# One core, a hybrid encoder block: splits and sums moved between GpSimd, VectorE and ScalarE at four places

## Chip, core and metric

The kernel runs on one core of one Trainium2 chip. The metric is the device time of one execution in microseconds (us). TensorE's clock has two levels, 1.2 and 2.4 GHz; the profile gives the granted clock as a share of the higher one. Engine names in rows: PE is TensorE, DVE is VectorE, ACT is ScalarE, POOL is GpSimd, SP is the sync engine, which issues most DMAs.

## The reference, cut to what matters

```python
h = _rms_norm(x, norm_mix_gain)                       # x is (1, 2048, 1024), float32
proj = h @ w_in                                       # q, k, v (768 columns each) and u (256)
attn = _dilated_attention(q, k, v, rel_bias_table)    # three windows and dilations, 12 heads
four = _fourier_mix(u, fourier_w, fourier_b)
x = x + concat(norm(attn), norm(four)) @ w_out
h = _rms_norm(x, norm_ffn_gain)
g, val = h @ w_gate, h @ w_val                        # D_FF = 2816
g = conv1d(g, conv_w) + conv_b                        # 3 taps along the positions
x = x + (silu(g) * val) @ w_down
return _rms_norm(x) * final_norm_gain
```

## The kernel before

Each float32 operand is split into two float16 parts, a high one (`hi`) and what it leaves (`lo`), and each product is three matmuls: hi·hi, hi·lo, lo·hi (`mm3`). Before a split, a tensor is scaled by a power of two that comes from its largest magnitude; finding it across partitions is a `PARTITION_ALL_REDUCE` on GpSimd (`all_max`). A split is an ACTIVATE on ScalarE (hi) and a subtraction (lo), on VectorE as one SCALAR_TENSOR_TENSOR that scales too (`split`), or on GpSimd as a TENSOR_TENSOR on data scaled beforehand. Every engine runs its own instructions in program order; pools give buffers and the waits on them.

- **Input projection** (`project`, 0 to some 180 us). The 2048 tokens go through in four quarters `c` of 512. For each there are four products V (values, two tokens blocks of 256 in halves `a`), two U (Fourier input) and sixteen Q (queries and keys). `hooks` lists, per quarter and product, which other work is emitted behind it. In quarter 0 the x rows 0 and 1 and rows 2 and 3 are normalized and turned apart (`half_turn`), the V weights `wv` are split partly on GpSimd, the Fourier weights `wf` and the first query and key weights `wqk` also.
- **Attention, Fourier, output projection** (to 1041.5 us, when the first gate product starts), not touched.
- **Gate and value tiles** (`glu`, 22 tiles `j`, to 1891.6 us). Seven half-size products stand for eight; `bank` holds X, Y, Z, W in PSUM, and `prod(n, a, b)` is 24 matmuls. Tile 20 also finds the last maxima of the down weights (`down_scale`, whose staging buffer `dws` is single) and starts the first down weights (`down_first`); tile 21 is `last_tile`, which ends in the largest magnitude `a_lm` that scales the down products.
- **Down, first half** (`down`, to 2010 us): 512 tokens, eleven steps `k` of two parts `i` with 24 matmuls each. During step `k` the weights of `k + 1` are split (`down_parts`) and their four sums made (`down_sums`) and split.
- **Down, second half** (to the end): 66 steps of 21 matmuls, seven products of three each; `last` adds the last seven up, normalizes and stores two blocks of 128 tokens.

Of the kernel before, what the change touches and what calls it, by code (L numbers as in the profile page):

```python
# [20 lines left out]
D = 1024  # L21
# [77 lines left out]
class Staged:  # L99
# [36 lines left out]

    def split(self, w, c0=0):
# [15 lines left out]
class Block:  # L153
# [47 lines left out]
    def rstd(self, ss, dim, name, unit2=None, width=None):  # L201
# [11 lines left out]
        nc.scalar.activation(y, v, AF.Sqrt)  # L213
        r = new("_r")
# [195 lines left out]
    def project(self, pv):  # L410
# [19 lines left out]
        def norm(c, js):  # L430
            r = self.rstd(stat[c][:, js[0]:js[-1] + 1], D, "xr", width=4)
            for i, j in enumerate(js):
                nc.vector.tensor_scalar(rows[c][j], rows[c][j], r[:, i:i + 1], None, op0=OP.mult)
# [3 lines left out]

        def half_turn(k, h):

            self.to_T([x[:, k * 128:(k + 1) * 128] for x in rows[0][2 * h:2 * h + 2]], self.hT, k, 1, R_MIX + k, self.mmtile,  # L440
                      2 * h, 2)
# [14 lines left out]
        load(0, (0, 1), nc.scalar)  # L456
# [4 lines left out]
        wv = self.staged("w_in", 2 * AW, "wv")  # L461
        load(0, (2, 3))
        wf = self.staged("w_in", 3 * AW, "wf")
# [4 lines left out]
        next(gains)  # L468
        wv.bound(w[:, 0])
        for k in range(KT):  # L470
            half_turn(k, 0)
            if k == 0:
                wv.root()
                nc.gpsimd.tensor_tensor(wv.st[:, 6:], wv.st[:, 6:], wv.s[:, 0:1, None].to_broadcast([128, 8 - 6, 256]),
                                        op=OP.mult)
            if k == 3:
                nc.scalar.activation(w[:, 0, :6], wv.st[:, :6], AF.Copy, scale=wv.s[:, 0:1])
            if k == 3:
                nc.vector.scalar_tensor_tensor(w[:, 1, :6], wv.st[:, :6], wv.s[:, 0:1], w[:, 0, :6], op0=OP.mult,
                                               op1=OP.subtract)  # L480
        nc.scalar.activation(w[:, 0, 6:], wv.st[:, 6:], AF.Copy)
        nc.gpsimd.tensor_tensor(w[:, 1, 6:], wv.st[:, 6:], w[:, 0, 6:], op=OP.subtract)
        squares(0, (2, 3))
        norm(0, (2, 3))


# [5 lines left out]

        def first_f():
            self.finv = self.const.tile([128, 1], F32, name="finv")
            nc.vector.tensor_copy(self.finv, wf.inv)
            wf.split(halves(W["f"]))

        def bound_f():
# [1712 lines left out]
```

## Time and profile before

| | |
|---|---|
| time, median of 3 runs | 2333.05 us (2329.04 to 2335.33) |
| the profiled execution: its time, and its span | 2329.35 us, 2327.5 us |
| TensorE busy | 2227.7 us, 96% of the span |
| VectorE, ScalarE, GpSimd busy | 71%, 43%, 31% |
| mean granted clock | 0.989 |

The span runs from the first to the last instruction; some 1.9 us lie around it. Busy shares are means over the whole; where a wait ends last is read stretch by stretch.

### The profile page before, as it was taken

To read this page: it belongs to the slowest core of one execution; us is meant where nothing else is said; L and a number is where in the kernel's file an instruction comes from. 1 tells how busy PE (TensorE), PEld (TensorE's weight loads), DVE (VectorE), ACT (ScalarE), POOL (GpSimd) and SP (SyncE) were. 2 spreads that over 40 slices of the span, in tenths; PEclk is the share of its full clock that TensorE was granted. 3 is DMA by queue.
4 is the path that set the end of the run, shared out by engine and by line. 5 is a ranking of instruction groups with operands and counts; after the bars stand their busy time and mean duration, and the time that the engine had idled before them with its cause. 6 is when DMAs were issued, how large, how long until landed. Compare 5 with 4: busy or idle time off the path is not lost.

```text
span 2327.5 us, 39297 instructions
## 1 busy us (share of the span) xinstructions
PE 2227.7 (96%) x15173; PEld 1199.0 (52%) x15173; DVE 1654.1 (71%) x3372; ACT 1007.4 (43%) x1841; POOL 730.7 (31%) x692
## 2 busy tenths in 40 slices
PE   5999999999999988999999999999999989999997
PEld 3657866666666654544444444444444434444443
DVE  4656768788787889863787877877778579654454
ACT  5433468677776764543222222222222144432222
POOL 1112122343443423231121221212212236566665
PEclk9999999999999998999999999999999999999998
DMA  3434334353543796960213222121221334443322
GB/s 134 144 102 125 119 105 122 81 139 84 156 124 111 219 286 201 276 178 13 73 55 100 68 78 91 46 91 57 80 91 46 100 118 136 135 137 96 95 91 82
DMA packets 281706, 266.47 MB, mean 114 GB/s; under 512 B 62102, under 2 KB 244014, under 8 KB 280494
## 3 DMA queue, kind: packets, MB, share of 16 engines
q1 hardware_dynamic: 276302, 245.60, 35.5%
q10 hardware_dynamic: 5216, 18.35, 2.2%
q8 instruction: 119, 1.95, 0.4%
q14 instruction: 69, 0.57, 0.1%
HBM read 176.32 MB, written 86.27 MB: 113 GB/s over the span
## 4 chain that ended last, share of the span: by engine, by line
issue 21%; PE 15%; POOL 9%; DVE 7%; ACT 4%; DMA 0%; POOLq 0%; ACTq 0%; SPq 0%; DVEq 0%
POOL A L1823 6%; PE d L241 4%; PE d L239 4%; PE d L240 4%; ACT A L1822 2%; PE X L1634 1%; DVE wst_v L1798 1%; DVE wd L192 1%; PE Z L1634 1%; ACT wd L191 1%; POOL sums L1908 1%; POOL sums L1907 1%; POOL sums L1906 1%; POOL sums L1905 1%; DVE wst_v L1802 0%
## 5 line engine op out<-in xcount | busy, mean ns | idle before, releaser
L1634 PEld LDWEIGHTS <-A 128*128 128x128 f16 x3744 | 366.6, 98 | 456.0 <-issue 16.2
L1002 ACT ACTIVATE s_sb<-s_sb,R 128x256 f32<-128x256 f32 (+1 forms) x576 | 229.7, 456 | 122.1 <-DVE R L994 121.4
L994 DVE CUSTOM_DVE_ANT_0 s_sb<-s,bias,alpha 128x256 f32<-128x256 f32 (+1 forms) x576 | 217.2, 420 | 77.6 <-PE s L989 76.9
L1634 PE MATMUL X<-h2T,A 128*128 128x512 f16 x1092 | 243.2, 379 | 1.7 <-DVE x L1529 1.7
L1634 PE MATMUL W<-h2T,A 128*128 128x512 f16 x984 | 220.6, 381 | 5.6 <-DVE gt L1728 5.6
L1634 PE MATMUL Y<-T,A 128*128 128x512 f16 x960 | 213.7, 379 | 4.5 <-DVE h2T L1653 2.2
L1823 POOL TENSOR_TENSOR A<-wst_v,A 128x2048 f16<-128x2048 f32 (+3 forms) x46 | 153.4, 3348 | 182.1 <-ACT A L1822 134.9
L241 PE MATMUL d<-wd,aT 128*128 128x512 f16 x540 | 204.7, 379 | 5.0 <-DVE aT L192 5.0
L239 PE MATMUL d<-wd,aT 128*128 128x512 f16 x540 | 204.7, 379 | 0.0
L240 PE MATMUL d<-wd,aT 128*128 128x512 f16 x540 | 204.7, 379 | 0.0
L192 DVE SCALAR_TENSOR_TENSOR aT<-wst_v,a_s,aT 128x896 f16<-128x896 f32 x66 | 86.9, 1316 | 145.6 <-ACT aT L191 145.6
L1014 DVE SCALAR_TENSOR_TENSOR pT<-pt,pT 128x512 f16<-128x512 f32 (+1 forms) x240 | 156.8, 653 | 15.9 <-ACT pT L1009 15.4
L191 ACT ACTIVATE aT<-wst_v,a_s 128x896 f16<-128x896 f32 x66 | 68.7, 1040 | 193.6 <-PE d L241 114.5
L165 POOL PARTITION_ALL_REDUCE wg_a<-am_g x22 | 8.2, 372 | 458.7 <-DVE am_g L1790 446.7
L241 PE MATMUL mm<-hT,wqk 128*128 128x512 f16 x384 | 146.4, 381 | 5.5 <-POOL wqk L642 5.5
L239 PE MATMUL mm<-hT,wqk 128*128 128x512 f16 x384 | 147.4, 384 | 2.7 <-ACT wqk L641 2.7
L1007 PE MATMUL pt<-eye,s_sb 128*128 128x128 f32 x900 | 148.0, 285 | 0.1
L1009 ACT ACTIVATE pT<-pt 128x512 f16<-128x512 f32 (+1 forms) x240 | 135.9, 566 | 24.7 <-PE pt L1007 16.0
L240 PE MATMUL mm<-hT,wqk 128*128 128x512 f16 x384 | 146.3, 381 | 0.0
L239 PE MATMUL av<-vb,pT 128*128 128x65 f16 (+1 forms) x960 | 116.3, 197 | 28.1 <-ACT R L1030 27.6
L1822 ACT ACTIVATE A<-wst_v 128x2048 f16<-128x2048 f32 (+3 forms) x46 | 73.1, 1593 | 158.0 <-DVE wst_v L1798 135.5
L1840 DVE SCALAR_TENSOR_TENSOR act<-gt,cw,act 128x2047 f32<-128x2047 f32 x22 | 81.9, 3723 | 60.4 <-ACT act L1837 60.4
(476 smaller groups left out, 4824.4 us busy)
## 6 DMA issues: line engine op xcount, KB each, us to landing
a_d<-val SPq DMA_DIRECT2D x42, 512.0 KB, 3.5
wst_v<-a_d SPq DMA_DIRECT2D x66, 256.0 KB, 3.3
vb<-v_d SPq DMA_DIRECT2D x12, 1040.0 KB
wst_v<-w_gate SPq DMA_DIRECT2D x22, 512.0 KB
wst_v<-w_val SPq DMA_DIRECT2D x44, 256.0 KB, 5.2
dws<-w_down SPq DMA_DIRECT2D x22, 512.0 KB, 6.0
wst_v<-w_down SPq DMA_DIRECT2D x11, 1024.0 KB, 5.0
Ro<-acc_d SPq DMA_DIRECT2D x36, 264.0 KB
```

The lines of the kernel that those rows point to most:

```text
L192: nc.vector.scalar_tensor_tensor(lo, src, scale, hi, op0=OP.mult, op1=OP.subtract)
L239: t.matmul(out, lh, rh, start=first, stop=False)
L240: t.matmul(out, lh, rl, start=False, stop=False)
L241: t.matmul(out, ll, rh, start=False, stop=last)
L994: nc.vector.tensor_tensor_reduce(s_sb[:, o:o + wd], s_ps[:, o:o + wd], bias[:, h, bc:bc + wd], alpha[:, 1:2], 3.0e38, OP.add, OP.min, nm)
L1002: nc.scalar.activation(s_sb[:, o:o + wd], s_sb[:, o:o + wd], AF.Exp, scale=-1.0, bias=nm)
L1007: nc.tensor.transpose(pt[:, o:o + 128], keep["p"][:, o:o + 128], self.eye)
L1009: nc.scalar.activation(pT[:, 0, :tot], pt[:, :tot], AF.Copy, scale=2.0 ** 14)
L1014: nc.vector.scalar_tensor_tensor(pT[:, 1, :tot], pt[:, :tot], 2.0 ** 14, pT[:, 0, :tot], op0=OP.mult, op1=OP.subtract)
L1634: nc.tensor.matmul(out[:, c - cols.start:c - cols.start + 512], A[:, a, x, k], B[b][:, y, k, c:c + 512], start=first and k == 0 and (x, y) ...
L1822: self.nc.scalar.activation(hi, src, AF.Copy)
L1823: self.nc.gpsimd.tensor_tensor(lo, src, hi, op=OP.subtract)
```

## The change

In the head all four x row tiles and both weight tiles are loaded by the ScalarE queue; the rows are turned 512 tokens at a time; `wv`, `wf` and the first `wqk` are scaled and split by ScalarE and VectorE alone (`direct`, `qk_direct`), and two small memsets go from GpSimd to VectorE. In gate tile 20 the sum that empties bank W stands ahead of the last `down_scale`. In `last_tile` the first down weights are split behind the first gate half (`next(first)`), the `a_max` part before the gate. In the first down half the four sums are made on VectorE, behind the splits; the x tiles are loaded one step part earlier than `load_f(2)`. In the last two steps of the down part the products of p1, p6, p7 and p5 go first, and `last` is written in another order with fewer GpSimd operations. Diff, cut (`down_sums` now takes the engine; `rstd` takes `during`; `half_turn` is gone):

```diff
+    def direct(self, w):
+        n, s = w.shape[2] // 2, self.s[:, 0:1]
+        for k in (slice(0, n), slice(n, 2 * n)):
+            self.b.nc.scalar.activation(w[:, 0, k], self.st[:, k], AF.Copy, scale=s)
+            yield
+            self.b.nc.vector.scalar_tensor_tensor(w[:, 1, k], self.st[:, k], s, w[:, 0, k], op0=OP.mult, op1=OP.subtract)
+            yield
...
         nc.scalar.activation(y, v, AF.Sqrt)
+        if during:
+            during()
...
-        load(0, (0, 1), nc.scalar)
+        load(0, range(4), nc.scalar)
         gains = self.gains(True)
         next(gains)
         self.eye = self.const.tile([128, 128], F32, name="eye")
         self.dma(self.eye, io["c_eye"])
-        wv = self.staged("w_in", 2 * AW, "wv")
-        load(0, (2, 3))
-        wf = self.staged("w_in", 3 * AW, "wf")
+        wv = self.staged("w_in", 2 * AW, "wv", nc.scalar)
+        wf = self.staged("w_in", 3 * AW, "wf", nc.scalar)
         next(gains)
         w = pv.tile([128, 2, KT, 256], F16, name="w_v")
         squares(0, (0, 1))
         norm(0, (0, 1))
-        next(gains)
+        squares(0, (2, 3))
+        norm(0, (2, 3), lambda: next(gains))
         wv.bound(w[:, 0])
+        first = [self.mmtile() for k in range(KT)]
+        for h in range(2):
+            for k in range(KT):
+                for j in (2 * h, 2 * h + 1):
+                    nc.tensor.transpose(first[k][:, j * 128:(j + 1) * 128], rows[0][j][:, k * 128:(k + 1) * 128], self.eye)
+        wv.root()
+        part = wv.direct(w)
         for k in range(KT):
-            half_turn(k, 0)
-            if k == 0:
-                wv.root()
-                nc.gpsimd.tensor_tensor(wv.st[:, 6:], wv.st[:, 6:], wv.s[:, 0:1, None].to_broadcast([128, 8 - 6, 256]),
-                                        op=OP.mult)
-            if k == 3:
-                nc.scalar.activation(w[:, 0, :6], wv.st[:, :6], AF.Copy, scale=wv.s[:, 0:1])
-            if k == 3:
-                nc.vector.scalar_tensor_tensor(w[:, 1, :6], wv.st[:, :6], wv.s[:, 0:1], w[:, 0, :6], op0=OP.mult,
-                                               op1=OP.subtract)
-        nc.scalar.activation(w[:, 0, 6:], wv.st[:, 6:], AF.Copy)
-        nc.gpsimd.tensor_tensor(w[:, 1, 6:], wv.st[:, 6:], w[:, 0, 6:], op=OP.subtract)
-        squares(0, (2, 3))
-        norm(0, (2, 3))
+            self.split(self.hT[:, 0, k, :512], self.hT[:, 1, k, :512], first[k], self.gs[:, R_MIX + k:R_MIX + k + 1])
+            if k % 2:
+                next(part)
+        load(1)
+        self.qk_load(0)
...
+        def bound_f():
+            W["f"] = xr.tile([128, 2, KT, 256], F16, name="wf")
+            wf.bound(W["f"][:, 0])
         def first_f():
+            wf.root()
             self.finv = self.const.tile([128, 1], F32, name="finv")
             nc.vector.tensor_copy(self.finv, wf.inv)
-            wf.split(halves(W["f"]))
-        def bound_f():
-            W["f"] = xr.tile([128, 2, KT, 256], F16, name="wf")
-            wf.bound(W["f"][:, 0]).root()
+            for _ in wf.direct(W["f"]):
+                pass
         def next_load():
             W["1"] = self.staged("w_in", 2 * AW + 256, "w1")
@@ -506,15 +513,15 @@
             W["1"] = W["1"].split(halves(pv.tile([128, 2, KT, 256], F16, name="w_v")))
         gains = self.gains(False)
-        at(0, "V", 0, bound_f, *(lambda k=k: half_turn(k, 1) for k in range(KT)))
-        at(0, "V", 1, lambda: next(gains), lambda: self.qk_load(0), lambda: load(1), wf.scale, first_f)
-        at(0, "V", 2, self.qk_bound)
-        at(0, "V", 3, lambda: self.qk_scale(0), lambda: self.qk_split(0, False), lambda: self.qk_split(1, False), lambda: next(gains))
+        bound_f()
+        at(0, "V", 0, first_f, lambda: next(gains))
+        at(0, "V", 1, self.qk_bound)
+        at(0, "V", 3, lambda: self.qk_scale(0, False), lambda: self.qk_direct(), lambda: next(gains))
         for c in range(3):
             if c:
                 at(c, "V", 0, lambda c=c: load(c + 1))
-            at(c, "V", 3, lambda c=c: squares(c + 1, range(4)))
-            at(c, "U", 0, lambda c=c: norm(c + 1, range(4)))
+            at(c, "V" if c else "U", 3 if c else 0, lambda c=c: squares(c + 1, range(4)))
+            at(c, "U", 0 if c else 1, lambda c=c: norm(c + 1, range(4)))
...
-                nc.gpsimd.memset(self.v_r[:, :, :, HD:HD + 1], 1.0)
-                nc.gpsimd.memset(self.v_r[:, :, :, VW - 1:VW], 0.0)
+                nc.vector.memset(self.v_r[:, :, :, HD:HD + 1], 1.0)
+                nc.vector.memset(self.v_r[:, :, :, VW - 1:VW], 0.0)
...
-        for i in range(2):
+        self.qk_s = s
+        for i in range(2 if weights else 0):
             nc.vector.tensor_scalar(st[:, i], st[:, i], s[:, i:i + 1], None, op0=OP.mult)
...
+    def qk_direct(self):
+        for i in range(2):
+            w, st, s = self.wq[i], self.qk_w[:, i], self.qk_s[:, i:i + 1]
+            self.nc.scalar.activation(w[:, 0], st, AF.Copy, scale=s)
+            self.nc.vector.scalar_tensor_tensor(w[:, 1], st, s, w[:, 0], op0=OP.mult, op1=OP.subtract)
...
+                prod("W", 6, "22")
+                tt_(u1, bank["W"], u1, op=add)
                 if j == NF - 2:
                     self.down_scale(gp, j + 1)
                     first = self.down_first()
                     next(first)
-                prod("W", 6, "22")
-                tt_(u1, bank["W"], u1, op=add)
                 past = self.glu_act(ga, j, gt, val, inv)
...
+            if n == "X":
+                next(first)
...
+        [*first]
...
-            if c == 1:
-                [*first]
...
-        _, ap = self.pow2(am[:, :NK], 0, "amx", NK)
+        am = self.all_max(am[:, :NK], "amx", NK)
+        yield
+        _, ap = self.pow2(am, 0, "amx", NK, reduced=True)
...
-                        self.down_sums(fs[k + 1], g)
-                        self.down_parts(k + 1, fs.pop(k + 1), w[k + 1], b12[k + 1])
+                        self.down_parts(k + 1, fs[k + 1], w[k + 1], b12[k + 1])
+                        self.down_sums(fs.pop(k + 1), g, nc.vector)
                     elif i == 0:
+                        x = [x_tile(t) for t in range(2)]
...
-                add(x2[:, hi], z)
+                onto(x2[:, hi], p5, x2[:, hi])
+                tt(x2[:, hi], x2[:, hi], z, op=OP.add)
+                square(0, x2[:, hi])
+                tt(x2[:, lo], x2[:, lo], z, op=OP.add)
                 onto(x1[:, hi], p5, x1[:, hi])
-                add(x2[:, lo], z)
-                onto(x2[:, hi], p5, x2[:, hi])
+                onto(x1[:, hi], p3, x1[:, hi])
+                square(1, x1[:, hi])
                 onto(x1[:, lo], p2, x1[:, lo])
-                onto(x1[:, hi], p3, x1[:, hi])
+                square(2, x1[:, lo])
                 onto(x2[:, lo], p4, x2[:, lo], neg)
-                for i, y in enumerate((x2[:, hi], x1[:, lo], x1[:, hi], x2[:, lo])):
-                    sq = other().bitcast(BF16)
-                    nc.scalar.activation(sq[:, :512], y, AF.Square, accum_out=ss[:, i:i + 1])
-                nc.gpsimd.tensor_tensor(x2[:, hi], x2[:, hi], fg[:, hi], op=OP.mult)
-                nc.gpsimd.tensor_tensor(x1[:, lo], x1[:, lo], fg[:, lo], op=OP.mult)
-                tt(x1[:, hi], x1[:, hi], fg[:, hi], op=OP.mult)
+                square(3, x2[:, lo])
+                for xi in (x2, x1):
+                    nc.gpsimd.tensor_tensor(xi[:, hi], xi[:, hi], fg[:, hi], op=OP.mult)
                 tt(sv, ss[:, 0:2], ss[:, 3:1:-1], op=OP.add)
-                nc.gpsimd.tensor_tensor(x2[:, lo], x2[:, lo], fg[:, lo], op=OP.mult)
                 r = self.rstd(sv, D, "xr")
                 for i, xi in enumerate((x2, x1)):
-                    nc.scalar.activation(xi[:, lo], xi[:, lo], AF.Copy, scale=r[:, i:i + 1])
-                    nc.vector.tensor_scalar(xi[:, hi], xi[:, hi], r[:, i:i + 1], None, op0=OP.mult)
+                    nc.scalar.activation(xi[:, hi], xi[:, hi], AF.Copy, scale=r[:, i:i + 1])
+                    stt(xi[:, lo], xi[:, lo], r[:, i:i + 1], fg[:, lo], op0=OP.mult, op1=OP.mult)
...
-                for i, (l, r) in enumerate(prods):
+                def prod(i, k, a):
+                    l, r = prods[i]
                     self.mm3(p[i], a[:, l, 0], a[:, l, 1], w[k][:, r, 0], w[k][:, r, 1], k == 0, k == NK - 1)
-                a = nxt
+                left = len(steps) - 1 - n
+                for i in range(7 if left > 1 else 4):
+                    prod(i, k, a)
+                if left == 0:
+                    for i in range(4, 7):
+                        prod(i, k - 1, before)
+                        prod(i, k, a)
+                before, a = a, nxt
...
```

The order of instructions at three places follows. GpSimd, from the start of the input projection to the first query and key weights; before (an ISA row stands where the kind of operation changes; `vrow` is the value row buffer):

```order
L474 ISA
L474 TENSOR_TENSOR wst_v<-wst_v,wv_s 128x512
L482 TENSOR_TENSOR w_v<-wst_v,w_v 128x512
L580 MEMSET vrow 128x8
L581 MEMSET vrow 128x8
L165 ISA
L165 ISA wf_a<-am_wf 128x1
L144 ISA
L144 TENSOR_TENSOR wf<-wst_v,wf 128x1024
L580 MEMSET vrow 128x8
L581 MEMSET vrow 128x8
L165 ISA
```

After the change, from the first ISA row of the same stretch to the all-reduce ahead of the output weights (`wo`):

```order
L174 ISA
L174 ISA gain_a<-gm 128x3
L174 ISA wv_a<-am_wv 128x1
L174 ISA wf_a<-am_wf 128x1
L174 ISA wqk_a<-am_qk 128x2
L174 ISA gain_a<-gm 128x3
L174 ISA wf_a<-am_f 128x1
L174 ISA wo_a<-am_o 128x1
```

All TENSOR_TENSOR and MEMSET rows have left GpSimd here; the all-reduces stand alone.

VectorE in gate tile 20, before (`gt` collects the gate, `dws` is the staged down weight, `am_d` joins the maxima):

```order
L1720 TENSOR_TENSOR gt<-Z,gt 128x1024
L1872 TENSOR_REDUCE wmax<-dws 128x1 x2
L1876 TENSOR_TENSOR am_d<-wmax 128x11
L1728 TENSOR_TENSOR gt<-W,gt 128x1024
L1830 TENSOR_SCALAR cw_20873<-vec,wg_i 128x3
```

After:

```order
L1735 TENSOR_TENSOR gt<-Z,gt 128x1024
L1888 TENSOR_REDUCE wmax<-dws 128x1
L1739 TENSOR_TENSOR gt<-W,gt 128x1024
L1888 TENSOR_REDUCE wmax<-dws 128x1
L1892 TENSOR_TENSOR am_d<-wmax 128x11
L1846 TENSOR_SCALAR cw_20845<-vec,wg_i 128x3
```

The sum out of bank W moved from behind both maxima and `am_d` to between the two maxima.

VectorE in the first down half, before; from the splits of step 1's weights `wd` to the split of their sums (`aT` is the split activation, `half` its source, `sums` the sums):

```order
L192 SCALAR_TENSOR_TENSOR wd_21274<-wst_v,wscl,wd_21274 128x512
L192 SCALAR_TENSOR_TENSOR other<-wst_v,wscl,other 128x512
L192 SCALAR_TENSOR_TENSOR wd_21274<-wst_v,wscl,wd_21274 128x2x512
L192 SCALAR_TENSOR_TENSOR aT<-half_21247,a_s,aT 128x512
L192 SCALAR_TENSOR_TENSOR wd_21274<-sums,wscl,wd_21274 128x4x512
```

After:

```order
L201 SCALAR_TENSOR_TENSOR wd_21246<-wst_v,wscl,wd_21246 128x512
L201 SCALAR_TENSOR_TENSOR other<-wst_v,wscl,other 128x512
L201 SCALAR_TENSOR_TENSOR wd_21246<-wst_v,wscl,wd_21246 128x2x512
L1921 TENSOR_TENSOR sums<-wst_v 128x512
L1922 TENSOR_TENSOR sums<-wst_v 128x512
L1923 TENSOR_TENSOR sums<-wst_v,sums 128x512
L1924 TENSOR_TENSOR sums<-sums,wst_v 128x512
L201 SCALAR_TENSOR_TENSOR aT<-half_21219,a_s,aT 128x512
L201 SCALAR_TENSOR_TENSOR wd_21246<-sums,wscl,wd_21246 128x4x512
```

Four TENSOR_TENSOR rows came in from GpSimd, between the last weight split and the next activation's.

## Rows read from the trace of the kernel before

**Rows 1.** Windows; length, busy PE, PEld, DVE, ACT, POOL, clock, DMA share, GB/s.
```profile
0.00:60.00 60.00, 36.05 (x188) 22.95 (x189) 25.90 (x87) 31.70 (x57) 10.58 (x17) 0.94 0.40 136
...
3.00:14.00 11.00, 4.38 (x17) 3.56 (x18) 5.62 (x27) 6.85 (x12) 0.79 (x2) 1.00 1.04 368
...
1834.80:1837.80 3.00, 2.95 (x8) 1.02 (x8) 0.78 (x2) 2.09 (x1) 0.00 (x0) 0.50 0.38 154
...
1957.97:1969.73 11.76, 10.62 (x50) 4.63 (x49) 10.24 (x6) 5.60 (x7) 7.18 (x4) 1.00 0.39 144
```

**Rows 2.** TensorE's waits over the whole span; total us, times, longest.
```profile
PE W L1634 <- DVE gt L1728: 5.6, 1, 5.6
...
PE mm L241 <- POOL wqk L642: 5.5, 1, 5.5
...
PE d L241 <- DVE aT L192: 5.3, 6, 1.2
...
PE W L1771 <- DVE a_lm L1769: 5.3, 1, 5.3
```

**Rows 3.** Timeline of GpSimd, first 60 us; start, length, [idle before <-releaser].
```profile
47.31 0.37 POOL L165 PARTITION_ALL_REDUCE wqk_a<-am_qk  x1 [9.29 <-issue]
...
54.81 4.19 POOL L642 TENSOR_TENSOR wqk<-wst_v,wqk 128x1024 f16<-128x1024 f32 x2 [7.14 <-ACT sq L428]
```

**Rows 4.** Timeline of TensorE in the first 62 us.
```profile
10.39 3.46 PE L344 MATMUL mm<-eye,x 128*128 128x128 f32 x15 [0.19 <-DVE x L433]
...
22.35 0.42 PE L241 MATMUL mm<-w_v,hT 128*128 128x256 f16 x1
...
56.98 0.61 PE L241 MATMUL mm<-hT,wqk 128*128 128x512 f16 x1 [5.49 <-POOL wqk L642]
...
59.79 0.38 PE L239 MATMUL mm<-hT,wqk 128*128 128x512 f16 x1
```

**Rows 5.** Timeline of ScalarE and of VectorE in the first 75 us.
```profile
9.32 1.91 ACT L124 ACTIVATE w_v<-wst_v 128x2048 f16<-128x2048 f32 x1 [1.43 <-DMA wst_v<-w_in]
...
67.67 4.70 DVE L192 SCALAR_TENSOR_TENSOR hT<-mm,gs,hT 128x512 f16<-128x512 f32 x7
```

**Rows 6.** Timeline of VectorE round gate tile 20's last sums.
```profile
1823.00 0.69 DVE L1802 TENSOR_TENSOR wst_v<-wst_v 128x512 f32<-128x512 f32 x1
...
1830.23 1.22 DVE L1872 TENSOR_REDUCE wmax<-dws 128x1 f32<-128x1024 f32 x1 [3.67 <-DMA dws<-w_down]
...
1833.59 1.21 DVE L1728 TENSOR_TENSOR gt<-W,gt 128x1024 f32<-128x1024 f32 x1
```

**Rows 7.** Timeline of GpSimd, TensorE and VectorE at the last gate tile.
```profile
1849.42 1.26 POOL L1905 TENSOR_TENSOR wst_v<-wst_v 128x512 f32<-128x512 f32 x1 [7.23 <-issue]
...
1880.40 2.75 PE L1634 MATMUL Z<-h2T,A 128*128 128x512 f16 x12
...
1883.82 0.74 DVE L1763 SCALAR_TENSOR_TENSOR val<-Y,wg_i,act 128x512 f32<-128x512 f32 x1
...
1891.58 0.61 PE L239 MATMUL d<-A,aT 128*128 128x512 f16 x1 [1.60 <-ACT aT L191]
```

**Rows 8.** Timeline of VectorE and ScalarE in the first down half.
```profile
1960.24 0.75 DVE L192 SCALAR_TENSOR_TENSOR aT<-half,a_s,aT 128x512 f16<-128x512 f32 x1
...
1960.90 1.76 DVE L192 SCALAR_TENSOR_TENSOR wd<-wst_v,wscl,wd 128x512 f16<-128x512 f32 x1
...
1967.70 2.00 ACT L191 ACTIVATE wd<-sums,wscl 128x2048 f16<-128x2048 f32 x1 [5.28 <-POOL sums L1908]
...
1969.73 2.35 DVE L192 SCALAR_TENSOR_TENSOR wd<-sums,wscl,wd 128x2048 f16<-128x2048 f32 x1 [1.52 <-ACT wd L191]
```

**Rows 9.** Timeline of TensorE and VectorE at the end of the kernel.
```profile
2313.41 0.38 PE L241 MATMUL d<-wd,aT 128*128 128x512 f16 x1
...
2314.47 2.73 DVE L2133 SCALAR_TENSOR_TENSOR xd<-d,a_C,xd 128x512 f32<-128x512 f32 x4 [0.47 <-POOL xd L2134]
...
2319.01 1.21 DVE L2155 TENSOR_TENSOR xsv<-xsl 128x2 f32<-128x2 f32 x1
```

More of the change, by code (lines that the diff above doesn't have):

```diff
@@ L199, in split_w, with rstd @@
         nc.gpsimd.tensor_tensor(lo, src, hi, op=OP.subtract)
-    def rstd(self, ss, dim, name, unit2=None, width=None):
+    def rstd(self, ss, dim, name, unit2=None, width=None, during=None):
         nc, sm = self.nc, self.small
@@ L428, in squares, with norm @@
                 nc.scalar.activation(sq, rows[c][j], AF.Square, accum_out=stat[c][:, j:j + 1])
-        def norm(c, js):
-            r = self.rstd(stat[c][:, js[0]:js[-1] + 1], D, "xr", width=4)
+        def norm(c, js, during=None):
+            r = self.rstd(stat[c][:, js[0]:js[-1] + 1], D, "xr", width=4, during=during)
             for i, j in enumerate(js):
@@ L436, in turn @@
             self.to_T([x[:, k * 128:(k + 1) * 128] for x in rows[c]], self.hT, k, 1, R_MIX + k, self.mmtile, 4 * c, 4)
-        def half_turn(k, h):
-            self.to_T([x[:, k * 128:(k + 1) * 128] for x in rows[0][2 * h:2 * h + 2]], self.hT, k, 1, R_MIX + k, self.mmtile,
-                      2 * h, 2)
         def fourier_in(c, j):
@@ L622, in new_wqk, with qk_scale @@
         return self.qkp.tile([128, 2, KT, 128], F16, name=f"wqk{i}")
-    def qk_scale(self, p):
+    def qk_scale(self, p, weights=True):
         nc, st = self.nc, self.qk_w
         s, inv = self.pow2(self.qk_m, 13, "wqk", 2, reduced=True)
-        for i in range(2):
+        self.qk_s = s
+        for i in range(2 if weights else 0):
             nc.vector.tensor_scalar(st[:, i], st[:, i], s[:, i:i + 1], None, op0=OP.mult)
@@ L1071, in channel_load @@
         self.wb = xr.tile([128, 2, 128], F32, name="wb")
-        nc.gpsimd.memset(self.wb, 0.0)
+        nc.vector.memset(self.wb, 0.0)
         for g in range(4):
@@ L1900, in down_parts, with down_sums @@
             self.split(hi, lo, src, self.wscl[:, k:k + 1])
-    def down_sums(self, f, g):
-        tt = self.nc.gpsimd.tensor_tensor
+    def down_sums(self, f, g, eng):
+        tt = eng.tensor_tensor
         tt(g[:, 0], f[:, 1], f[:, 0], op=OP.subtract)
@@ L1915, in down_first @@
         g = self.wst.tile([128, KT, 256], F32, name="wst_v").rearrange("p (s k) n -> p s (k n)", s=4)
-        self.down_sums(f, g)
+        self.down_sums(f, g, nc.gpsimd)
         yield
@@ L2057, in down @@
                         self.dma(fg, sub(io["final_norm_gain"], 0, [[0, 128], [1, D]]))
-                        x = [x_tile(t) for t in range(2)]
                     elif k + 1 < NK:
@@ L2136, in last, with square @@
                 ss, sv = sm.tile([128, 4], F32, name="xsl"), sm.tile([128, 2], F32, name="xsv")
+                def square(i, y):
+                    sq = other().bitcast(BF16)
+                    nc.scalar.activation(sq[:, :512], y, AF.Square, accum_out=ss[:, i:i + 1])
                 nc.scalar.activation(u, p1, AF.Copy, scale=unit)
```

## Prediction

> **What bounds the kernel now.** The page first: TensorE is busy 96% of the span at a mean clock of 0.989. A gain can only come from the few places where it idles or runs slowly, so next come its waits over the whole span [rows 2]. Four stand out, one in each part that the change touches: bank W (5.6 us), the first query and key matmul behind a GpSimd split (5.5), the first down half behind VectorE's splits (5.3 in six waits), and the last magnitude `a_lm` (5.3). The windows view then shows what a list of waits hides [rows 1]: in the first 60 us TensorE is busy for 36.1 us, so it idles 24; DMA is busy 0.40 there, and only in the stretch from 3 to 14 us saturated (368 GB/s). Behind the W wait the granted clock is 0.50, the 1.2 GHz level, for 3 us.
>
> **Head.** Removed: GpSimd's multiplications, subtractions and memsets. What they cost isn't their own time: the all-reduce of `wqk` takes 0.37 us but starts after 9.29 idle us that no other engine explains, and the split of `wqk` after another 7.14 [rows 3]. Such gaps stand where the kind of operation changes; when only all-reduces are left, as the order shows, there is none. Before, TensorE does its first V products at the low clock (the matmul at 22.35 shows 0.42 us, the later ones 0.27, both with their drain), waits for rows 2 and 3, and starts Q late: the tenth Q matmul starts at 59.79 [rows 4]. Nine matmuls at the full rate (0.216 each, start to start) ahead of it would be a start at 57.85. That is the mark to compare with.
>
> After: 32 transposes at the 0.213 of [rows 4] (3.46 for 15, less the drain) from 10.4 on end near 17.3. `wv` stands behind two more x tiles, 1 MB, in one queue: at 368 GB/s [rows 1] 2.8 us more at worst; from an issue start near 2.5, 3 MB are there at about 11, against 9.3 before, when ScalarE's `bound` of it starts [rows 5]. With 1.9 for `bound`, an all-reduce of 0.4 and six small operations, the scale is ready near 15. VectorE then does eight hT splits of 0.67 [rows 5] and two weight halves of about 1.2 (half the 2.35 of a 2048 wide one [rows 8]): 15.1 + 5.4 + 2.4 and some waits for ScalarE's halves give 23.6. Until then some 13 of the 96 V matmuls can run. The other 83 at 0.108 are 9.0 (to 32.6), 48 U matmuls at 0.216 another 10.4 (to 43.0). The low clock costs more: behind the W wait it lost 1.5 us [rows 1]; for the longer idle here I allow 0 to 3.4 and take 1.9, a little over that row. Q starts at 44.9: **12.9 gained**, 11.2 to 14.7. The covers: `wf` is split on ScalarE and VectorE behind the hT splits, some 5 us of work under 9 us of V; `wqk` is loaded ahead of V, and has its maxima, scale and splits under V and U.
>
> A rule of the Trainium skill speaks against the move of the loads ("DMA: Bandwidth & Descriptors", Issuing engines are not separate DMA queues): transfers that ScalarE starts run on the same sixteen engines and interleave with all others, so another issuer saves only issue time. No run here shows the interleaving of the new queue; if `wv` came in with `wf`, 1 MB later, the sum would lose 2.8 us of the 12.9.
>
> **Tile 20.** Before, `gt<-W` starts at 1833.59, behind two maxima and `am_d`; the first maximum waits 3.67 us for a DMA into the single buffer `dws` [rows 6]. That is the 5.6 of [rows 2]. It now stands behind the first maximum alone. What is late next: the products of tile 21 need its split weights and bank Z. Both are there about when TensorE asks, so 4.4 to 5.6 is gained; I take 5.6. The low clock behind it goes too: 3.0 us at half rate [rows 1] did 1.5 us of work: 1.5, at least 0. At the other end Z's matmuls end near 1883.1, and the first down product starts at 1891.58 [rows 7]. VectorE comes to `val` only at 1883.82, after the last splits and the `amx` scale; three `val` and maximum pairs then run in a row, 1.38 us each, of which two should be done by then. They go under the products: 2.2, between 1.2 (one) and 3.2 (one and a half more). Against it: the down splits and the all-reduce now stand ahead of the gate's activation; if GpSimd is late there, the gate is. **9.3 gained**, 6.0 to 10.3.
>
> **First down half.** A step lasts 11.76 us, in which TensorE is busy 10.62, with its drain [rows 1]; 48 matmuls at 0.216 are 10.36. The wait is for the chain: GpSimd's sums, ScalarE's split of them (2.00, after 5.28 idle us for POOL), VectorE's (2.35) [rows 8]. On VectorE a split of 512 takes 0.75 (0.66 start to start) when GpSimd is idle, and 1.76 beside GpSimd's sums [rows 8]: the two disturb each other. Without GpSimd: three 512 splits at 0.66 (2.0), the double one 1.2, four sums at 0.62 (2.5; such a sum takes 0.69 with drain [rows 6]), the second `aT` and the wait for ScalarE's sums 2.15, their lo part 2.3: 10.1 us, under 10.36. The waits go: **5.3 gained**; 2.5 if a third of a microsecond a step stays, at most 5.6. The earlier x tiles: 0.3, at least 0.
>
> A rule of the Trainium skill ("SBUF — State Buffer", Who interferes with whom) has VectorE and GpSimd share one pair of ports as an exclusive lock; the trace's 1.76 against 0.75 agrees. By it alone the four sums run undisturbed, and the sum keeps its 5.3.
>
> **Tail.** The last matmul starts at 2313.41. Behind it four additions on VectorE (2.73 us, drain included), squares, `sv` at 2319.01, the root, the last scale and the store run to the end of the span, 2327.5 [rows 9]. After, p1, p6, p7 and p5 are complete 27 to 18 matmuls ahead of the end, so only p3, p2 and p4 are left, and `sv` ends about 1.8 to 3 us sooner; the gain product merges into the last scale. **3.0 gained**, 1.8 to 4.4.
>
> **Sum.** 12.9 + 9.3 + 5.3 + 0.3 + 3.0 = 30.8. TensorE is the bound in between, so the head's gain should reach the end whole; some half a microsecond may be lost on the way, so 30.3. The profiled execution took 2329.35: 2299.0. It lies 3.7 under the median of 2333.05; against the median, 2302.7. I say 2302, since three runs spread by 6 us.
>
> **Rivals.** What a measurement of this kernel can tell from no change is about 0.3%, 7 us.
> - *VectorE becomes the bound of the first down half.* It now does all splits and sums. If each sum takes the 1.71 of the disturbed rate (1.76 in [rows 8] is its like) instead of 0.62, four more microseconds a step: 14.5 against 10.36, ten steps, 41 over the forecast's steps: 2303 + 41 = 2344, slower. The point that decides is a step of 13.4 us: ten of them lose the 30.3 that the rest gains. For it: VectorE is already near full there, 10.24 of 11.76 us [rows 1]. Against it: the long durations stand only beside GpSimd, which is now idle. A middle case, 11.0 a step, gives 2303 + 6.4 = 2309.
> - *The last gate tile comes late.* The all-reduce stands behind GpSimd's sums with a gap of 7 to 9 us [rows 3, 7]; then the gate's activation and the products of tile 21's second half wait, and 3 to 6 us of the 9.3 are lost: 2305 to 2308. The Trainium skill ("GPSIMD Engine Reference", Instruction dispatch) says that the first call of a freshly loaded kernel pays a load of about 6 us; the gaps of 7.14 to 9.29 are of that kind, and longer.
> - *The head's gain is lost further down.* If the next quarter's x or the later query and key weights land late, TensorE waits there and 10 of 12.9 go: 2313. The DMA share of 0.40 in the head [rows 1] speaks against it.
> - *Nothing changes.* Each removed wait would have to return in another place: 2333. No row points to that.
>
> **How the numbers follow.** The forecast as summed, with the bounds of its terms (21.5 to 35.3 gained if every term fell on one side; 25 to 34 as they mix): 0.70, 2299 to 2308. Late gate or middle down step: 0.16, 2305 to 2309. Head lost: 0.07. Nothing: 0.04. Slower: 0.03. The likeliest is 2302; the range from 2294 (all terms at their upper ends, 35.3 off the profiled execution) to 2312 leaves out the last three cases, 0.14 together, and little of the rest. Faster by over 0.3% takes all but the last two: 0.93; same 0.04; slower 0.03.
>
> **What would show it.** Q's matmuls starting near 45 (head); no wait for `wqk` or POOL there; no W wait, TensorE's gap behind the last gate tile near 6 in place of 8.4, with the clock at full behind tile 20; steps of 10.4 us in the first down half, VectorE's sums at 0.6 to 0.7; and 11 us or less from the last matmul to the end of the span, where it is 14.1 now. Wrong would be VectorE sums above 1.2 us, a new wait for GpSimd's `amx` ahead of the last gate, or waits for DMA between 60 and 200 us that weren't there.

## Result and the profile after

The changed kernel takes 2306.61 us (median of 4 runs, 2301.61 to 2311.19), the kernel before, beside it, 2334.19 (2329.04 to 2337.23): a ratio of 0.9879, interval 0.9853 to 0.9905, 27.6 us less. The forecast was 2302. Its profiled execution took 2309.21 us, with a span of 2307.4 against 2327.5. Seen in pieces, between landmarks in TensorE's timeline of the two profiled executions (us):

| stretch | before | after | gained | forecast |
|---|---|---|---|---|
| to Q's start (before: nine full-rate matmuls ahead of the tenth) | 57.85 | 43.78 | 14.1 | 12.9 |
| Q's tenth matmul to the first attention matmul | 235.69 | 242.65 | -7.0 | 0 |
| to the first gate product | 746.05 | 752.34 | -6.3 | 0 |
| to the first down product | 850.05 | 840.39 | 9.7 | 9.3 |
| to the last matmul | 421.83 | 416.02 | 5.8 | 5.6 |
| to the end of the span | 14.09 | 10.28 | 3.8 | 3.0 |

These add up to 20.1, the difference of the spans. The four places that the change was made for gained a little more than was forecast, 33.4 us where 30.8 were summed; two stretches in which nothing was expected gave 13 us back.

TensorE's waits in the changed kernel, over the span (total us, times, longest):

```profile
PE av L250 <- ACT R L1045: 25.2, 27, 5.2
...
PE s L1004 <- DVE vrow L201: 6.9, 1, 6.9
PE t L1512 <- issue: 5.5, 1, 5.5
...
PE W L1787 <- DVE a_lm L1785: 1.9, 1, 1.9
```

All four waits of [rows 2] are gone or small: none for W, for `wqk` behind GpSimd, or for `aT` behind VectorE, and `a_lm` (the last magnitude, of the down products) is down from 5.3 to 1.9. What is new stands at the start of attention, `s` behind VectorE's value row: 6.9.

The timelines of VectorE, GpSimd and TensorE there (start, length, [idle before <-releaser]):

```profile
279.54 0.07 DVE L587 MEMSET vrow<- 128x8 f16 x1 [7.67 <-DMA v_d<-vrow]
...
279.61 8.04 DVE L721 TENSOR_SCALAR bias<-bias,alpha 128x512 f32<-128x512 f32 x3
287.57 1.11 DVE L201 SCALAR_TENSOR_TENSOR vrow<-mm,vrow 128x256 f16<-128x256 f32 x3
...
274.62 12.09 POOL L701 COPY k<-k 128x1024 f16<-128x1024 f16 x8
...
281.19 0.27 PE L252 MATMUL mm<-wo_s,hT 128*128 128x256 f16 x1
288.37 1.29 PE L1004 MATMUL s<-k,q 64*64 64x128 f16 x18 [6.90 <-DVE vrow L201]
```

and the durations of the three bias multiplications by themselves (the view of the tile: shortest/median/longest in ns), after the change and then before:

```profile
L721 DVE TENSOR_SCALAR bias<-bias,alpha x3: 342/474/7384, 279.6 to 287.3; 128x512 f32<-128x512 f32 x2, 128x256 f32<-128x256 f32 x1
```

```profile
L706 DVE TENSOR_SCALAR bias<-bias,alpha x3: 353/486/820, 288.4 to 289.6; 128x512 f32<-128x512 f32 x2, 128x256 f32<-128x256 f32 x1
```

One multiplication stands for 7.4 us, to 287.0, while GpSimd copies keys until 286.7; value rows queue behind it on VectorE, and TensorE, whose last value product starts at 281.19, waits for them. Before, GpSimd came to those copies only later. Its timeline there, before:

```profile
293.97 0.13 POOL L580 MEMSET vrow<- 128x8 f16 x1 [5.07 <-DMA v_d<-vrow]
...
294.71 0.13 POOL L580 MEMSET vrow<- 128x8 f16 x1 [0.58 <-DMA v_d<-vrow]
...
294.79 6.28 POOL L686 COPY k<-k 128x1024 f16<-128x1024 f16 x5
```

The value row memsets stood ahead of them, and waited there for a store. The change moved these memsets to VectorE, and nothing held the copies any more.

The wait costs more than its 6.9 us. Behind it the granted clock is at its lower level, and TensorE needs 4.52 us for the first 28 matmuls of attention, where it needed 3.03 before. The windows (length, busy PE, PEld, DVE, ACT, POOL, clock, DMA share, GB/s), after the change and then before:

```profile
288.37:292.89 4.52, 4.52 (x28) 1.99 (x28) 2.08 (x11) 1.60 (x4) 0.00 (x0) 0.51 0.82 234
```

```profile
295.48:298.51 3.03, 2.90 (x28) 1.26 (x29) 1.82 (x10) 2.89 (x6) 3.03 (x4) 1.00 0.71 206
```

These 1.5 us stand in the next stretch of the table, so the price at the start of attention is 8.4 us in all.

### The profile page after: what moved, and what is told of

Read it like the earlier page. It is cut to its first block, busy times and chain, and to the rows that moved or that the text cites. A ratio compares the mean times of both kernels' runs of the same rounds, so it can differ in the third digit from the quotient of the medians.

```text
span 2307.4 us, 39210 instructions
## 1 busy us (share of the span) xinstructions
PE 2225.1 (96%) x15173; PEld 1199.9 (52%) x15173; DVE 1648.1 (71%) x3455; ACT 1007.6 (44%) x1833; POOL 648.3 (28%) x595
## 4 chain that ended last, share of the span: by engine, by line
PE 25%; issue 18%; POOL 6%; DVE 5%; ACT 2%; DMA 0%; POOLq 0%; DVEq 0%; ACTq 0%
PE d L250 6%; PE d L252 6%; PE d L251 6%; POOL A L1839 5%; PE X L1649 3%; PE Z L1649 2%; PE Y L1649 2%; PE W L1649 2%; ACT A L1838 1%; DVE wst_v L1814 1%; DVE wst_v L1818 0%; DVE wst_v L1822 0%; DVE wst_v L1824 0%; DVE wst_v L1823 0%; PE Y L1662 0%
## 5 line engine op out<-in xcount | busy, mean ns | idle before, releaser
L251 PEld LDWEIGHTS <-pT 128*128 128x128 f16 (+1 forms) x960 | 86.7, 99 | 58.3 <-issue 35.9
```

Of the source, the lines that this page charges most:

```text
L251: t.matmul(out, lh, rl, start=False, stop=False)
```

## Experiments

Theory A for the 7.0 us is that the key copies, set free by the moved memsets, hold VectorE up in the bias multiplication; the rival, theory B, that the value row's store is what everything waits for. Further edits undo the change's parts one by one, to see what each is worth. All are edits of the changed kernel. Each time is compared with the kernel before, run beside it. Where single stretches are given, they come from one profiled execution each, by the landmarks of the table above. In the table below "to attention" runs from Q's tenth matmul to the first attention matmul, "to gate" from there to the first gate product, and so on, in us.

| kernel | median us | ratio (interval) | Q's tenth | to attention | to gate | to down | to last | to end |
|---|---|---|---|---|---|---|---|---|
| after_again | 2309.16 | 0.9901 (0.9874 to 0.9927) | 46.70 | 242.41 | 746.62 | 840.85 | 415.08 | 10.24 |
| bias_act | 2296.99 | 0.9849 (0.9821 to 0.9877) | 45.85 | 238.41 | 746.12 | 839.08 | 415.00 | 10.84 |
| memset_pool | 2300.74 | 0.9857 (0.9830 to 0.9885) | 46.53 | 237.82 | 751.10 | 839.72 | 415.51 | 10.22 |
| head_before | 2311.87 | 0.9912 (0.9881 to 0.9944) | 60.35 | 238.80 | 754.05 | 840.51 | 415.49 | 10.30 |
| sums_pool | 2313.56 | 0.9911 (0.9877 to 0.9944) | 46.98 | 243.19 | 749.43 | 840.87 | 420.58 | 10.25 |
| w_behind | 2314.74 | 0.9899 (0.9876 to 0.9923) | 45.15 | 246.20 | 750.66 | 845.70 | 415.70 | 10.29 |
| first_between | 2310.24 | 0.9885 (0.9858 to 0.9911) | 47.59 | 242.94 | 752.51 | 845.67 | 414.93 | 10.56 |
| tail_before | 2314.91 | 0.9900 (0.9867 to 0.9933) | 47.60 | 245.13 | 756.96 | 838.37 | 415.28 | 14.06 |
| pool_beside | 2332.92 | 0.9988 (0.9973 to 1.0003) | 47.12 | 242.61 | 750.35 | 841.84 | 436.19 | 10.29 |
| wv_sp | 2309.21 | 0.9874 (0.9843 to 0.9906) | 45.53 | 242.65 | 744.03 | 840.07 | 415.60 | 10.32 |
| qk_pool | 2307.09 | 0.9867 (0.9840 to 0.9895) | 45.17 | 245.05 | 745.61 | 842.05 | 415.54 | 10.28 |
| sums_first | 2310.51 | 0.9880 (0.9853 to 0.9907) | 48.38 | 245.44 | 750.38 | 839.99 | 415.97 | 10.34 |

The kernel before took 2331.54 us beside the first four (6 runs of each), 2338.85 beside the next four (4 runs) and 2336.14 beside the last four (4 runs, 10 of pool_beside).

**Is the new wait part of the change?** after_again, no edit.

> The changed kernel once more, nothing edited. Theory A: the 6.9 us that TensorE waits ahead of the first attention matmul come with the change (VectorE's first bias multiplication stands still while GpSimd copies keys), so the wait is there again, 6 to 7.5 us. Theory B: it was an accident of one execution; then it is gone or a few us off. The wait of 5.5 us at the transposes of the output projection is expected to move or change in size: the transposing DMAs there vary between executions. Time 2302 to 2311 us.

The wait for the value row is there again (7.1), and again, 6.9 to 7.5, in each of the eight later profiles in which VectorE scales the bias while GpSimd has no memsets ahead of its copies. The wait of 5.5 in the output projection is not: that stretch took 746.6 instead of 752.3.

**What holds VectorE?** Two edits take the same wait away in different ways. bias_act moves the multiplications:

```diff
-        self.nc.vector.tensor_scalar(self.bias[p, b], self.bias[p, b], self.al[p][:, 2:3], None, op0=OP.mult)
+        if p:
+            self.nc.vector.tensor_scalar(self.bias[p, b], self.bias[p, b], self.al[p][:, 2:3], None, op0=OP.mult)
+        else:
+            self.nc.scalar.activation(self.bias[p, b], self.bias[p, b], AF.Copy, scale=self.al[p][:, 2:3])
```

> The three bias multiplications ahead of attention go from VectorE to ScalarE. Theory A (VectorE's bias multiplication stands still beside GpSimd's key copies, and the value evacuations queue behind it): the 6.9 us wait falls to 1.5 or less, attention starts near 282, and the kernel takes 4 to 7 us less than the changed one. Theory B (the wait hangs on the value store, which lands at 279.5, for which the memset waits): 5 us or more of the wait remain, time as the changed kernel's.

memset_pool leaves them on VectorE and puts GpSimd's old work back ahead of the copies:

```diff
-                nc.vector.memset(self.v_r[:, :, :, HD:HD + 1], 1.0)
-                nc.vector.memset(self.v_r[:, :, :, VW - 1:VW], 0.0)
+                nc.gpsimd.memset(self.v_r[:, :, :, HD:HD + 1], 1.0)
+                nc.gpsimd.memset(self.v_r[:, :, :, VW - 1:VW], 0.0)
```

> The two small memsets of each value row buffer go back from VectorE to GpSimd, all else as changed. Theory A: the memsets hold GpSimd until the store has landed, the key copies start behind them, VectorE's bias multiplications take 0.4 to 0.9 us and the wait of 6.9 falls to 2 or less; in the head GpSimd's gaps come back, but Q still starts before 46, since the key weights have 9 us to spare; 3 to 6 us less than the changed kernel. Theory C (the gaps decide in the head): Q starts 5 us or more later and nothing is won.

The change moves a third memset too, that of `wb` in `channel_load`; it stays on VectorE here.

In both, the wait is gone. GpSimd and VectorE in bias_act:

```profile
277.56 12.21 POOL L701 COPY k<-k 128x1024 f16<-128x1024 f16 x8
...
282.38 0.07 DVE L587 MEMSET vrow<- 128x8 f16 x1 [7.65 <-DMA v_d<-vrow]
...
282.75 0.76 DVE L201 SCALAR_TENSOR_TENSOR vrow<-mm,vrow 128x256 f16<-128x256 f32 x2 [0.27 <-ACT vrow L200]
```

The memset waits for the store as long as before (7.65), and the copies run beside it: theory B, the store, falls, since nothing is lost by it. Without the bias on VectorE the value rows follow at once. In memset_pool the three multiplications take 2.28 us together, and the copies start behind them:

```profile
276.56 2.28 DVE L721 TENSOR_SCALAR bias<-bias,alpha 128x512 f32<-128x512 f32 x3 [1.74 <-DMA bias<-bias_d]
...
283.67 12.32 POOL L701 COPY k<-k 128x1024 f16<-128x1024 f16 x8
```

Theory A holds. bias_act is 12.2 us below after_again and memset_pool 8.4, both more than was expected; the wait of 7.1 and the slower clock behind it (4.38 us instead of 3.03, 1.4) make 8.5, and with runs that spread by 10 us the rest is not to be read. bias_act beats both kernels. In it attention started at 284.26, later than the 282 expected: TensorE's wait for the table `tw` before it was 3.0 instead of 1.5, with a slower clock behind it (0.96 mean from 140 to 180 us, 1.00 in after_again).

**How much of the head reaches the end?** head_before brings back the old head: loads, `half_turn`, splits and all three memsets on GpSimd. Its edit, cut:

```diff
...
+            if k == 0:
+                wv.root()
+                nc.gpsimd.tensor_tensor(wv.st[:, 6:], wv.st[:, 6:], wv.s[:, 0:1, None].to_broadcast([128, 8 - 6, 256]),
+                                        op=OP.mult)
...
+        at(0, "V", 3, lambda: self.qk_scale(0), lambda: self.qk_split(0, False), lambda: self.qk_split(1, False), lambda: next(gains))
...
```

> The changed kernel with the input projection's head of before (loads, half turns, splits on GpSimd, memsets on GpSimd). Q's tenth matmul is at 59 to 60 again, 14 us later, but the 6.9 us wait ahead of attention is gone: 7 us more than the changed kernel, about 2313 (2311 to 2316). If the head's 14 us reached the end whole, 2320.

Q's tenth matmul is 13.7 us later, the stretch to attention 3.6 shorter (the wait is gone, a wait of 2.6 for `tw` and a slower clock are in it). The time, 2.7 us more, is too small a difference for runs that overlap; its own profiled execution has 7.4 us more in the untouched stretch to the gate. The comparison that answers the question is with memset_pool, which has the new head and, like head_before, no wait at attention: there attention starts 14.8 us earlier (284.35 against 299.15), and the median is 11.1 us lower, with no run of one among those of the other (2291.66 to 2302.89, 2305.79 to 2321.29). Without the collision the head's gain does reach the end.

**The parts of the head.** wv_sp gives the weights back to the sync engine's queue, qk_pool the low parts of `wqk` to GpSimd.

```diff
-        wv = self.staged("w_in", 2 * AW, "wv", nc.scalar)
-        wf = self.staged("w_in", 3 * AW, "wf", nc.scalar)
+        wv = self.staged("w_in", 2 * AW, "wv")
+        wf = self.staged("w_in", 3 * AW, "wf")
```

> The changed kernel with the V and Fourier weights loaded by the sync engine again, the four x tiles on ScalarE's queue. Order decides (one queue keeps x ahead of the weights): now weights and x interleave, the second pair of x tiles comes 1 to 3 us later, V weights earlier, Q's tenth matmul between 44 and 48. If the queue made no difference at all: 45.7 to 46.7 as in the two profiles of the changed kernel.

```diff
-        at(0, "V", 3, lambda: self.qk_scale(0, False), lambda: self.qk_direct(), lambda: next(gains))
+        at(0, "V", 3, lambda: self.qk_scale(0), lambda: self.qk_split(0, False), lambda: self.qk_split(1, False), lambda: next(gains))
```

> The changed kernel with the low parts of the first query and key weights made on GpSimd again (scaled by VectorE first). Theory A of the head (GpSimd's gaps of 7 to 9 us cost what TensorE waits): GpSimd's first subtraction starts 6 to 8 us behind its all-reduce and is done near 41 to 43, about as Q wants it: 0 to 3 us later, and the key copies come later too. Theory B (it is the early loads and turns that give the 14 us): Q's tenth matmul at 46 to 47, no wait for POOL, since V and U now cover the gap.

Neither makes Q later (45.53 and 45.17 against 45.72 and 46.70). For wv_sp both expectations hold at 45.53, so it shows only that the queue of these two loads is worth little here. VectorE's last V split and Q's first matmul in the changed kernel:

```profile
22.92 1.27 DVE L143 SCALAR_TENSOR_TENSOR w_v<-wst_v,wv_s,w_v 128x1024 f16<-128x1024 f32 x1
...
43.78 0.38 PE L250 MATMUL mm<-hT,wqk 128*128 128x512 f16 x1
```

GpSimd in qk_pool:

```profile
30.80 0.41 POOL L174 PARTITION_ALL_REDUCE wqk_a<-am_qk  x1 [6.93 <-ACT wqk L625]
38.78 4.21 POOL L650 TENSOR_TENSOR wqk<-wst_v,wqk 128x1024 f16<-128x1024 f32 x2 [7.57 <-ACT sq L439]
```

The gap ahead of GpSimd's subtraction is back, 7.57 us, about as long as in [rows 3]. But the all-reduce is 16.5 us earlier than there, and the subtractions end at 43.0, just before Q wants them. So this gap costs nothing once the weights come early, and theory A falls for it. That the early loads and turns give the 14 us, theory B, is what is left; qk_pool does not try them by themselves.

**First down half.** sums_pool undoes the engine and the order, sums_first only the order:

```diff
-                        self.down_parts(k + 1, fs[k + 1], w[k + 1], b12[k + 1])
-                        self.down_sums(fs.pop(k + 1), g, nc.vector)
+                        self.down_sums(fs[k + 1], g, nc.gpsimd)
+                        self.down_parts(k + 1, fs.pop(k + 1), w[k + 1], b12[k + 1])
```

> The changed kernel with the four sums of the first down half on GpSimd again, ahead of the splits. Theory A (the two engines' disturbance made the wait): VectorE's 512 wide splits take 1.7 to 1.8 beside GpSimd's sums, TensorE waits for aT 5 to 6 us in all, and the stretch from the first down product to the second half is 5 to 6 us longer; whole kernel 5 to 6 us more. Theory B (the order alone, splits ahead of sums, was what helped): 2 us or less.

> The changed kernel with the four sums of a step, still on VectorE, ahead of the weight splits instead of behind them. If the engine alone matters: period 10.37 us, no wait, 415 to 416 us from the first down product to the last matmul. If the order matters: ScalarE's splits are done earlier than VectorE's low parts are, aT of the second part comes up to 1 us late in a step, 1 to 5 us more.

The stretch is 420.58 with the sums on GpSimd, 415.97 with them on VectorE ahead of the splits, 416.02 in the changed kernel: the engine matters, the order doesn't. VectorE in sums_pool, and then in the changed kernel:

```profile
1949.33 1.76 DVE L201 SCALAR_TENSOR_TENSOR wd<-wst_v,wscl,wd 128x512 f16<-128x512 f32 x1
```

```profile
1937.45 0.74 DVE L201 SCALAR_TENSOR_TENSOR wd<-wst_v,wscl,wd 128x512 f16<-128x512 f32 x1
...
1940.20 0.68 DVE L1921 TENSOR_TENSOR sums<-wst_v 128x512 f32<-128x512 f32 x1
```

**The rival that ends slower, at its price.** pool_beside adds GpSimd work that nothing uses beside VectorE's, in each step:

```diff
+                        g2 = dp.tile([128, 256], F32, name="spare")
+                        for y in range(8):
+                            z = slice(y % 2 * 256, (y % 2 + 1) * 256)
+                            nc.gpsimd.tensor_tensor(g2, fs[k + 1][:, y // 2, z], fs[k + 1][:, 3 - y // 2, z], op=OP.subtract)
```

> The changed kernel, with extra work that nothing uses: in each of the ten steps of the first down half GpSimd makes eight 256 wide differences of the same weights into a spare buffer, beside VectorE's splits and sums. The rival of the prediction (VectorE disturbed becomes the bound) at its price: VectorE's 512 wide operations beside GpSimd take 1.2 to 1.8 us instead of 0.6 to 0.75, its round goes from 8.8 busy to 12 to 14 us, a step from 10.37 to 12 to 14, 16 to 36 us more from the first down product to the last matmul. If VectorE isn't disturbed when it reads along: under 2 us more.

VectorE and GpSimd in it:

```profile
1936.27 0.75 DVE L201 SCALAR_TENSOR_TENSOR aT<-half,a_s,aT 128x512 f16<-128x512 f32 x1
...
1941.54 1.21 DVE L1922 TENSOR_TENSOR sums<-wst_v 128x512 f32<-128x512 f32 x1
...
1949.35 0.75 DVE L201 SCALAR_TENSOR_TENSOR aT<-half,a_s,aT 128x512 f16<-128x512 f32 x1
...
1937.19 9.54 POOL L2072 TENSOR_TENSOR spare<-wst_v 128x256 f32<-128x256 f32 x8 [3.54 <-DMA wst_v<-w_down]
```

A sum takes 1.21 us instead of 0.68, VectorE's round 13.08 instead of 10.37, and the stretch is 20 us longer; the kernel is no longer clearly faster than the one before (ratio 0.9988). The prediction put the step at which the whole gain is lost at 13.4. Ten steps of 13.08 would have lost 27 us in the stretch; 20 were lost, since VectorE had a lead at first (TensorE's second and third step still took 10.36 and 11.05 us). The rival's mechanism is real, though it put a sum at 1.71 and a step at 14.5; what it needed, GpSimd busy beside VectorE, was not there.

**The last gate tiles.** w_behind and first_between undo one step each.

```diff
-                prod("W", 6, "22")
-                tt_(u1, bank["W"], u1, op=add)
                 if j == NF - 2:
...
                     next(first)
+                prod("W", 6, "22")
+                tt_(u1, bank["W"], u1, op=add)
```

> The changed kernel with bank W's product and sum of gate tile 20 behind the last down_scale again. The step's claim: a wait of 5 to 6 us at W, behind it 3 us at a granted clock of 0.5, and 7 us more between the first gate product and the first down product (840.4 in the changed kernel). If only the wait counts and the clock falls anyway elsewhere: 5.5 us.

```diff
-            if n == "X":
-                next(first)
...
-        [*first]
...
+            if c == 1:
+                [*first]
```

> The changed kernel with the first down weights' splits and their scales between the last gate's products again. The step's claim: the wait for a_lm is 5 us instead of 1.9, and 2 to 3.5 us more between the first gate product and the first down product. Rival: if the down weights aren't split until VectorE gets to them, the activation of the last gate comes earlier and nothing is lost: 1 us or less.

w_behind has a wait of 3.7 at W, a slower clock behind it and a stretch that is 5.3 longer. TensorE's wait, and 6 us behind it (columns as above) in w_behind and then in the changed kernel:

```profile
PE W L1649 <- DVE gt L1743: 3.7, 1, 3.7
```

```profile
1834.00:1840.00 6.00, 5.50 (x18) 2.18 (x18) 3.75 (x3) 2.09 (x1) 1.37 (x1) 0.72 0.57 175
```

```profile
1834.00:1840.00 6.00, 6.00 (x30) 2.70 (x28) 3.96 (x2) 1.98 (x1) 0.20 (x1) 1.00 0.32 131
```

first_between has the wait for `a_lm` of 5.3 again; TensorE from the last gate product on, in it and then in the changed kernel:

```profile
1877.54 2.75 PE L1649 MATMUL Z<-h2T,A 128*128 128x512 f16 x12
...
1888.71 0.61 PE L250 MATMUL d<-A,aT 128*128 128x512 f16 x1 [1.60 <-ACT aT L200]
```

```profile
1873.60 2.75 PE L1649 MATMUL Z<-h2T,A 128*128 128x512 f16 x12
...
1881.10 0.61 PE L250 MATMUL d<-A,aT 128*128 128x512 f16 x1 [1.60 <-ACT aT L200]
```

11.17 against 7.50 us, from the start of Z's last group: 3.7.

**Tail.** tail_before brings back the order of the products and sums of before. Its edit, cut:

```diff
...
-                for i in range(7 if left > 1 else 4):
-                    prod(i, k, a)
...
+                for i, (l, r) in enumerate(prods):
+                    self.mm3(p[i], a[:, l, 0], a[:, l, 1], w[k][:, r, 0], w[k][:, r, 1], k == 0, k == NK - 1)
...
```

> The changed kernel with the products of the last two steps and the last sums in the order of before. The step's claim: from the last matmul to the end of the span 13.5 to 14.5 us instead of 10.3, 3 to 4 us more in all; VectorE's four last additions end 1 us or more later behind the last matmul.

From the last matmul to the end 14.06 against 10.28: 3.8. The last matmul and `sv` in the changed kernel:

```profile
2297.12 0.38 PE L252 MATMUL d<-wd,aT 128*128 128x512 f16 x1
...
2299.81 0.16 DVE L2178 TENSOR_TENSOR xsv<-xsl 128x2 f32<-128x2 f32 x1 [0.85 <-ACT other L2158]
```

## Why the prediction held, and where it did not

The time lies within the range, 4.6 us above the forecast, and for the main part by the steps given. In part that is luck: 8.4 us were lost at the start of attention, where half a microsecond was allowed for, and terms that were put 2.6 us too small made up for some of it.

- **Head.** Q was forecast at 44.9 and started at 43.78, and the chain (32 turns, VectorE's splits, 9.0 us of V, 10.4 of U) is the one in the profile: VectorE's last V split runs from 22.92 to 24.19, the forecast had its end at 23.6. The 1.9 us allowed for the low clock did not come in this execution, where the mean granted clock from 25 to 45 us is 1.00. Where it is 1.00 Q's tenth matmul starts at 45.15 to 45.85 (five profiles), where it is 0.93 to 0.96 at 46.53 to 47.12 (four), and where it is 0.89 to 0.91 at 47.59 to 48.38 (three). So Q's start goes with the clock, and the 14.1 lies near the upper end of 11.4 to 14.6. What the text gave as the cause is only partly right: GpSimd's gaps need not all be gone. With the one ahead of the `wqk` split back, Q starts no later (qk_pool), and neither does it with the weights on the other queue (wv_sp). Which of the rest, the earlier load of the key weights, the 512 wide turns or the V splits off GpSimd, gives how much of the 14 us was not tried apart.
- **The step that failed.** "TensorE is the bound in between, so the head's gain should reach the end whole; some half a microsecond may be lost on the way, so 30.3." Over half of it, 8.4 of 14.1, was lost at the start of attention: 6.9 of waiting and 1.5 by the slower clock behind it. The prediction has no term for the moved memsets, though it lists them among what leaves GpSimd; what they had held up there, the key copies behind them, was not asked. Moved back (memset_pool), they take the wait away. The rival of the lost head gain had 0.07, named late loads and put the loss at 10; the loss came instead by two engines getting in each other's way.
- **Tile 20 and the last gate tile.** Together 9.7 measured, 9.3 forecast, with errors that seem to cancel: the W step was put at 7.1 and is worth 5.3 when it is undone, since the wait is then 3.7, not 5.6, and the slower clock behind it costs 1.7 (0.72 for 6 us). That 5.3 is loose, as the stretch took 838.4 to 842.1 us in the eleven profiles in which nothing in it was undone. The end was put at 2.2 with 3.2 as its bound and is worth 3.7. Both `val` pairs ahead of Z's (1.38 us each) went under the products, as said, and VectorE is also free when Z's matmuls end, where it came 0.7 us late: the middle of the bounds was no good guide to a sum of two things that both happen. The clock behind tile 20 is full after the change, as forecast (1.00 from 1824 to 1836 us). GpSimd's gap of 7.17 us ahead of its sums did not make the gate late, so the rival of the late gate tile falls. The lower bound of this part was added up wrong (4.4, 0 and 1.2 make 5.6, not 6.0); nothing hangs on it.
- **First down half.** 5.8 against 5.6, by the named mechanism: no wait, steps of 10.37 us and sums of 0.68 us. The step of 11.76 that the prediction started from is not that of the whole half: before, TensorE's steps took 10.36 us from the second to the seventh and 11.7 to 12.3 from the eighth to the eleventh, while VectorE's round took 10.80 us from the start and 11.77 later. VectorE's round was the longer one all along, and TensorE felt it only when VectorE's lead was used up. So the waits of 5.3 were the right measure of the gain, and a longer step can't be priced by ten of it, as the rival did.
- **Tail.** 3.8 against 3.0; the term that was mis-sized is `sv`, put at 1.8 to 3 us sooner: it ends 2.85 us behind the start of the last matmul, where 6.81 us passed before [rows 9].
- **The untouched stretch.** From attention to the gate, profiled executions took 744 to 757 us with the same code there. In the changed kernel's profile the squares of the output projection waited 17.6 us in four waits, in that of before 8.0 in three. The profile puts 4.3 of the 17.6 down to the transposing DMA that reads their buffer and 13.3 to nothing that it shows; these DMAs' issues took 1.7 to 8.0 us there. That they cause the spread was argued from these rows, not tried. Of the 6.3 us lost here, 1.5 come from the slower clock at the start of attention; the rest is within this spread.

## What to carry to other kernels

When an instruction is taken off an engine, ask what it was holding up: work behind it will start earlier, and may run into another engine's. A wait that costs nothing by itself can keep two engines apart. And read a change stretch by stretch between landmarks: here the runs spread by 10 us, while the stretches that parts of the change touch repeat within 4.

## What was not expected of the hardware

VectorE and GpSimd disturb each other in two ways. Beside GpSimd's two-input TENSOR_TENSOR, VectorE's operations slow to 1.2 or 1.76 us from 0.7. Beside its eight copies, one VectorE TENSOR_SCALAR of 512 columns stood 7.4 us and ended 0.3 us after the last copy, while the memsets just ahead of it took 0.07 each. In all ten profiles with this order it took 7.4 to 8.1 us and ended 0.3 us after the last copy. The Trainium skill ("SBUF — State Buffer", Who interferes with whom) says that a `tensor_scalar` can take the pair of ports which VectorE shares with GpSimd, and that the one that comes second then blocks fully until the other's instruction is finished. The trace agrees on the block; but each copy is an instruction of its own (the last four take 2.0 us each), and VectorE stood to the end of the fourth of these, not of one.
